# First modulation of a two-layer trunk: adaLN weights as TensorE's stationary operand, and the opening written out anew

## The chip, the cores and the metric

One Trainium2 chip, one of its cores. The time of a kernel is the device time of one launch in microseconds (us), given as the median of several runs; before and after are compared on it.

## What is computed

The program is a two-layer diffusion trunk (layer 0 an mLSTM mixer, layer 1 latent attention, a gated ConvFFN after each) on 256 latent and 256 context tokens of width 1024. Each sub-layer reads its input through a modulation that depends on a condition vector, `c` for the latent tokens and `c_ctx` for the context:

```python
def _modulation(cond, w, b):
    m = jax.nn.silu(cond) @ w + b          # (1024,) @ (1024, 6*1024)
    return jnp.split(m[:, None, :], 6, axis=-1)

def _modulate(x, shift, scale):
    return x * (1 + scale) + shift
...
ml = _modulation(c, ada_w[i], ada_b[i])
mc = _modulation(c_ctx[None, :], ada_w[i], ada_b[i])
hl = _modulate(x, ml[0], ml[1])
hc = _modulate(xc, mc[0], mc[1])
...
x_m = h @ w_up                             # the mLSTM's first product
```

The change touches only the first of these: shift and scale of layer 0, two times 1024 numbers for each of the two conditions, and the first product behind them, `h @ w_up`. Nothing of layer 0 can begin before shift and scale are there.

## The kernel before

All products of float32 data are made on TensorE from a rounded type (`F32R`): an operand is split into a high part (a cast on ScalarE, called ACT in the profile) and a low part (a subtraction on VectorE, called DVE), and three products high*high, high*low, low*high are summed. A matmul of plain `F32` operands also exists and needs no split.

**The opening** (`start_up`) computes shift and scale and the first `NUP` = 6 of the 16 column blocks of `h @ w_up`. It goes by eight blocks of 128 features, f = 0 to 7. For a block it loads the weights of the modulation (`adaw`), the transposed tokens `xT` (128 features x 512 tokens), and a row block `raw0` of `w_up` (128 x 768). Then:

- `rows`: the product of the conditions with the block's modulation weights. The two condition columns are the stationary operand and the weights stream, so the result `adar` is a row, two (or, split in high and low, four) partitions high. For f = 0 and 1 (`F32T`) the operands are plain float32; for the others the weights are split first (`hi` on ACT, `lo` on DVE, into `adas`) and the split condition `condr` is used.
- For f < `NFD` = 4, shift and scale of the block both come from these rows (256 columns); for f of 4 and above only the shift does (128 columns), and the scale comes from two multiply-and-sum instructions on DVE (`sum`, line L589) over a transposed copy `adat`.
- `copy` takes the row out of PSUM, `T` transposes it on TensorE back into PSUM, and `cols` adds the bias, which gives columns `mod0`, one number per feature and condition.
- `h` and `xx` apply shift and scale to the tokens (`h` rounded into `hT`, `xx` in float32), once for each half g of the tokens; `hlo` makes the low part. `whi` and `wlo` split the block of `w_up`.
- `up`f,i: the i-th of the three products of block f, six matmuls of 128 x 512, one into each of six PSUM banks that stay open through the opening. There are 8 x 3 x 6 = 144 of them (L745).

The order in which these steps are put on TensorE, DVE, ACT and SP's load queue is written out by hand, in the list `PLAN`; each engine then runs its own instructions in that order. SP's queue holds the loads of f = 0 to 3, the two condition rows `bc`, the loads of f = 4, and those of f = 5, 6, 7, which come when `wlo`0, 1, 2 stand in the list. Behind the opening comes `w_up`, the remaining ten column blocks (L458 to L460), and then the rest of the trunk, whose order a scheduler makes.

`Z`n issues n matmuls of a zero tile (L723), which compute nothing; `Z7` stands at the head of the list.

Of the kernel before, what the change touches and what calls it, by code (L numbers as in the profile page):

```python
# [8 lines left out]
F32R = mybir.dt.float32r  # L9
I32 = mybir.dt.int32  # L10
AF = mybir.ActivationFunctionType
ALU = mybir.AluOpType
# [5 lines left out]
T = SEQ + CTX  # L18
# [13 lines left out]
NB, NRAW, NU, NS = 3, 3, 31, 15  # L32
# [16 lines left out]

NUP = 6  # L50
NFD = 4
F32T = (0, 1)
PLAN = """
Z7 rows00 rows01 whi0 wlo0 copy0 T0 rows10 cols0 h00 h01 xx00 xx01 rows11 hlo0 up02 copy1 whi1 hi200 T1
up00 cols1 h10 hi210 lo200 up01 h11 wlo1 whi2 up10 lo210 hi300 rows20 wlo2 hi310 rows21 lo300 up12 copy2
lo310 whi3 xx11 T2 rows30 cols2 xx10 h21 rows31 h20 xx21 xx20 wlo3 up22 copy3 hi400 hlo2 T3 hlo1 silu0
up21 cols3 h30 silu1 lo400 up11 whi4 sum40 h31 rows40 hi500 sum41 up20 xx31 copy4 lo500 up32 whi5 xx30
hlo3 T4 rows50 cols4 wlo4 h41 up31 h40 sum50 hi600 up30 xx40 lo600 xx41 up42 copy5 hlo4 hi700 rows60 sum51
T5 up41 cols5 lo700 h51 copy6 up40 whi6 wlo5 xx51 sum60 rows70 h50 T6 sum61 copy7 up52 xx50 hlo5 up50
cols6 wlo6 h60 T7 up51 h61 sum70 whi7 xx60 up62 sum71 xx61 cols7 up60 hlo6 h70 wlo7 h71 up61 xx70 xx71  # L60
up72 hlo7 up70 up71
""".split()

TAIL = {"mout": 4, "aout": 7, "fout1": 6}
# [365 lines left out]
class K:  # L430
# [63 lines left out]
    def setup(self):  # L494
        nc, p = self.nc, self.pool
        a = self.a
        self.sm = p.tile([128, a["sm"].shape[1]], F32, name="sm")
        nc.sync.dma_start(self.sm[:, :32], a["sm"][:, :32])
        b1 = self.smc("ada_b")[:, 8:16]
        nc.vector.tensor_scalar(b1, b1, 1.0, None, op0=ALU.add)  # L500
        jp = p.tile([128, 128], I32, tag="s2", name="jp", bufs=NS)
        nc.gpsimd.iota(jp, pattern=[[1, 128]], base=0, channel_multiplier=-1)
        self.ident = p.tile([128, 128], F32, name="ident")
        nc.vector.tensor_scalar(self.ident, jp, 0.0, None, op0=ALU.is_equal)
        self.mask = p.tile([128, 2, 128], F32, name="mask")
        nc.vector.tensor_scalar(self.mask[:, 0], jp, 0.0, NEG, op0=ALU.is_gt, op1=ALU.mult)
        nc.vector.tensor_scalar(self.mask[:, 1], jp, 0.0, NEG, op0=ALU.is_lt, op1=ALU.mult)
        self.k1 = p.tile([128, 1], F32, name="k1")
        nc.vector.memset(self.k1, 1.0)
        self.zero = p.tile([128, 512], F32R, tag="s2", name="zero", bufs=NS)  # L510
        nc.vector.memset(self.zero.bitcast(F32), 0.0)
        self.keps = p.tile([128, 1], F32, name="keps")
        nc.vector.memset(self.keps, EPS)
        self.cond = p.tile([128, 8, 2], F32, name="cond")
        nc.scalar.activation(self.cond.rearrange("p a b -> p (a b)"), self.smc("cond"), AF.Silu)
        self.condr = p.tile([128, 8, 4], F32R, name="condr")
        self.split(self.condr[:, :, 0:2], self.condr[:, :, 2:4], self.cond)
        self.mod0 = p.tile([128, 2, 8, 2], F32, name="mod0")
        self.modc = {(0, c): self.mod0[:, c] for c in range(2)}
        self.gd = {}  # L520
        self.adav = p.tile([128, 32], F32, name="adav")
        nc.vector.memset(self.adav, 0.0)
        for l in range(2):
            for c in (3, 4) if l == 0 else (0, 1, 3, 4):
                self.modc[l, c] = p.tile([128, 8, 2], F32, name="mod%d%d" % (l, c))
            for c in (2, 5):
                self.gd[l, c] = self.dr.tile([2, D], F32, name="gd%d%d" % (l, c))

    def ada_hi(self, f, h, q):
        self.adas[f, h] = [self.pool.tile([128, 1024], F32R, tag="u", name="adas", bufs=NU) for _ in range(2)]  # L530
        self.nc.scalar.copy(self.adas[f, h][0], self.adaw[f, h])

    def ada_lo(self, f, h, q):
        hi, lo = self.adas[f, h]
        self.nc.vector.tensor_sub(lo, self.adaw.pop((f, h)), hi)

    def ada_rows(self, f, h):

        nc = self.nc
        nh = 2 if f < NFD else 1  # L540
        n = 128 * nh
        if h == 0:
            self.adap[f] = self.ps("adar")
        pr = self.adap[f]
        m = 8 // nh
        for k in range(h * m, (h + 1) * m):
            c = slice((k - h * m) * n, (k - h * m + 1) * n)
            if f in F32T:
                nc.tensor.matmul(pr[0:2, 0:n], self.cond[:, k, :], self.adaw[f, h][:, c], start=k == 0, stop=k == 7)
                continue  # L550
            for i, x in enumerate(self.adas[f, h]):
                nc.tensor.matmul(pr[0:4, 0:n], self.condr[:, k, :], x[:, c],
                                 start=k == 0 and i == 0, stop=k == 7 and i == 1)
        del (self.adaw if f in F32T else self.adas)[f, h]

    def ada_copy(self, f):
        n = 256 if f < NFD else 128
        q = 2 if f in F32T else 4
        self.adar[f] = r = self.s2("adarow")
        (self.nc.vector.tensor_copy if f == 0 else self.nc.scalar.copy)(r[0:q, 0:n], self.adap[f][0:q, 0:n])  # L560

    def ada_T(self, f):
        r = self.adar.pop(f)
        q = 2 if f in F32T else 4
        for i in range(2 if f < NFD else 1):
            self.nc.tensor.transpose(self.adap[f][:, 256 + q * i:256 + q * i + q], r[0:q, i * 128:(i + 1) * 128],
                                     self.ident[0:q, 0:q])

    def ada_cols(self, f):
        nc = self.nc  # L570
        p = self.adap.pop(f)[:, 256:]
        b = self.smc("ada_b").rearrange("p (c f) -> p c f", c=2)[:, :, f:f + 1]
        if f in F32T:
            nc.vector.tensor_tensor(self.mod0[:, :, f, :], p[:, 0:4].rearrange("p (c b) -> p c b", c=2),
                                    b.to_broadcast([128, 2, 2]), op=ALU.add)
            return
        n = 2 if f < NFD else 1
        m = self.mod0[:, 0:n, f, :]
        p = p[:, 0:4 * n].rearrange("p (c x b) -> p c x b", c=n, x=2)
        nc.vector.tensor_tensor(m, p[:, :, 0], b[:, 0:n].to_broadcast([128, n, 2]), op=ALU.add)  # L580
        nc.vector.tensor_tensor(m, p[:, :, 1], m, op=ALU.add)

    def ada_sum(self, f, j):

# [101 lines left out]
    def start_up(self):  # L686

        nc, st = self.nc, self.st
# [3 lines left out]
        self.t2d = {(p, j): self.dr.tile([128, 1024], F32, name="t2d") for p in range(2) for j in range(4)}  # L692
        self.xA, self.x1, self.xc, self.xcr = {}, {}, [], []
        w, raws = [], []
        self.adaw, self.adas, self.adap, self.adar, self.adat, self.xT = {}, {}, {}, {}, {}, []

        def load(f):
            if f < NFD:
# [57 lines left out]
        def silu(j):  # L756
            nc.scalar.activation(self.bc[j], self.bc[j], AF.Silu)

        ops = {"Z": warm, "rows": self.ada_rows, "copy": self.ada_copy, "T": self.ada_T, "cols": self.ada_cols,
               "hi": self.ada_hi, "lo": self.ada_lo, "sum": self.ada_sum, "silu": silu, "whi": w_hi, "wlo": w_lo,  # L760
               "h": h, "xx": lambda f, g: self.mod_part(f, g, self.xT[f]), "hlo": hlo, "up": up}
        e = mybir.EngineType
        with self.tc.manual_schedule(engines={e.PE, e.DVE, e.Activation, e.SP}):
# [4 lines left out]
            for t in PLAN:  # L768
                name = t.rstrip("0123456789")
# [1500 lines left out]
```

## Time and profile before

| | us |
|---|---|
| time, median of 3 runs | 1356.97 (1356.48 to 1357.79) |
| the profiled execution's own time | 1356.08 |
| its span in the profile | 1354.3 |
| from the first matmul that computes something to the first of `w_up` | 5.18 to 57.14 |

The profiled execution took 1.78 us more than its span, and 0.89 us less than the median. In the profile PE is TensorE's matmuls, PEld its loads of the stationary operand, SPq the load queue of SP. A plain float32 matmul leaves two records of a load and a matmul each in the trace, one of the rounded type leaves one. In the columns of a group, out<-in names the tiles, then come partitions x elements; for TensorE "128*2" stands for rows x columns of the stationary operand, and the shape behind it is what streams or is loaded. The ends of matmuls are modelled, so how fast they follow each other is read from their starts.

### The profile page before, as it was taken

What the parts mean: (1) busy time and instruction counts of PE and PEld (TensorE: products, weight loads), DVE (VectorE), ACT (ScalarE), POOL (GpSimd) and SP (SyncE); (2) the same over time, 40 slices, a digit from 0 to 9 for tenths busy, and PEclk for the clock granted to TensorE, in tenths of its full rate; (3) what the DMA queues carried; (4) which work ended last, traced back from release to release, by engine and by line L of the source; (5) the groups of instructions that cost most, each with busy time, mean ns of one, the idle gap of its engine ahead of it and who ended that gap; (6) DMA issues with size and microseconds to landing.
All of it is one profiled execution on the core that took longest, in us unless ns stands there. A gap on an engine that the chain in (4) does not pass through costs nothing.

```text
span 1354.3 us, 18733 instructions
## 1 busy us (share of the span) xinstructions
PE 1342.8 (99%) x6649; PEld 1126.8 (83%) x6649; DVE 1081.7 (80%) x1786; ACT 716.4 (53%) x1249; POOL 123.1 (9%) x216
## 2 busy tenths in 40 slices
PE   9999999999999999999999999999999999999997
PEld 6888888888788888888898888888888988988886
DVE  6898866687688696877789887778887898898884
ACT  5685443435444455374654333343458757676661
POOL 0032000011011010120002000000100011000100
PEclk9999999999999999999999999999999999999999
DMA  9799848789656373765747677775877425476850
GB/s 366 241 302 311 293 171 262 233 281 297 230 191 205 124 233 116 244 200 184 236 142 259 217 249 224 244 228 170 246 262 246 133 74 165 140 219 200 263 189 31
DMA packets 88093, 291.96 MB, mean 216 GB/s; under 512 B 11640, under 2 KB 12280, under 8 KB 88000
## 3 DMA queue, kind: packets, MB, share of 16 engines
q1 hardware_dynamic: 61840, 215.64, 48.7%
q0 software_dynamic: 17520, 57.70, 13.8%
q10 hardware_dynamic: 8640, 17.44, 3.4%
q8 instruction: 52, 0.85, 0.3%
q14 instruction: 41, 0.34, 0.1%
HBM read 260.15 MB, written 30.58 MB: 215 GB/s over the span
## 4 chain that ended last, share of the span: by engine, by line
PE 92%; DMA 4%; DVE 2%; ACT 1%; issue 0%; SPq 0%; DVEq 0%; ACTq 0%
PE fin L459 6%; PE fin L460 6%; PE fin L458 6%; PE tok L459 6%; PE tok L460 6%; PE tok L458 6%; PE y L1667 5%; PE fin L1578 5%; PE qk L458 4%; PE qk L460 4%; PE qk L459 4%; PE y L459 4%; PE y L458 4%; PE y L460 4%; PE fin L1583 3%; DMA raw<-in_ws 2%
## 5 line engine op out<-in xcount | busy, mean ns | idle before, releaser
L374 DVE TENSOR_TENSOR w<-raw,w 128x1024 fp32r<-128x1024 f32 (+1 forms) x256 | 307.5, 1205 | 111.4 <-ACT w L371 109.1
L371 ACT CAST w<-raw 128x1024 fp32r<-128x1024 f32 (+1 forms) x256 | 265.3, 1038 | 244.7 <-PE tok L460 86.3
L610 DVE SCALAR_TENSOR_TENSOR junk<-ar,bc 128x1024 f32<-128x1024 f32 x128 | 155.8, 1217 | 7.3 <-ACT bc L647 5.0
L459 PE MATMUL fin<-h,w 128*128 128x512 f32 (+1 forms) x376 | 141.2, 376 | 0.0
L458 PE MATMUL fin<-h,w 128*128 128x512 f32 (+1 forms) x376 | 141.2, 376 | 0.0
L460 PE MATMUL fin<-h,w 128*128 128x512 f32 (+1 forms) x376 | 141.1, 375 | 0.0
L458 PE MATMUL qk<-xc,w 128*128 128x512 f32 x256 | 100.5, 392 | 0.0
L460 PE MATMUL qk<-xc,w 128*128 128x512 f32 x256 | 99.7, 390 | 0.0
L459 PE MATMUL qk<-xc,w 128*128 128x512 f32 x256 | 99.6, 389 | 0.0
L459 PEld LDWEIGHTS fin<-h,w 128*128 128x128 f32 x376 | 70.8, 188 | 13.0
L458 PEld LDWEIGHTS fin<-h,w 128*128 128x128 f32 x376 | 70.7, 188 | 13.0
L460 PEld LDWEIGHTS fin<-h,w 128*128 128x128 f32 x376 | 70.7, 188 | 12.6
L1578 PE MATMUL fin<-h,w 128*128 128x512 f32 x312 | 78.1, 392 | 0.0
L1578 PEld LDWEIGHTS fin<-h,w 128*128 128x128 f32 x312 | 56.1, 189 | 10.0
L458 PEld LDWEIGHTS qk<-xc,w 128*128 128x128 f32 x256 | 48.1, 188 | 10.1 <-issue 0.4
L460 PEld LDWEIGHTS qk<-xc,w 128*128 128x128 f32 x256 | 48.0, 188 | 10.1
L459 PEld LDWEIGHTS qk<-xc,w 128*128 128x128 f32 x256 | 48.1, 188 | 9.8
L784 ACT ACTIVATE fg<-fg 128x512 f32<-128x512 f32 (+1 forms) x44 | 23.0, 525 | 58.7 <-DVE fg L782 52.5
L458 PE MATMUL tok<-w,hT 128*128 128x512 f32 x128 | 49.8, 389 | 0.0
L459 PE MATMUL tok<-w,hT 128*128 128x512 f32 x128 | 49.8, 389 | 0.0
L460 PE MATMUL tok<-w,hT 128*128 128x512 f32 x128 | 49.8, 389 | 0.0
L1667 PE MATMUL y<-w,fz 128*128 128x512 f32 x198 | 46.2, 392 | 0.4 <-DVE w L374 0.4
(495 smaller groups left out, 3257.0 us busy)
## 6 DMA issues: line engine op xcount, KB each, us to landing
raw<-in_ws SPq DMA_DIRECT2D x281, 512.0 KB, 4.7
ar<-in_adaT SPq DMA_DIRECT2D x80, 512.0 KB, 4.6
raw<-in_ws POOLq DMA_DIRECT2D x13, 512.0 KB, 7.7
raw<-in_ws SPq DMA_DIRECT2D x12, 384.0 KB, 8.3
adaw<-in_adaf SPq DMA_DIRECT2D x8, 512.0 KB, 6.6
xmd<-xr POOLq DMA_DIRECT2D x16, 256.0 KB, 4.9
xcd<-cv POOLq DMA_DIRECT2D x16, 256.0 KB, 5.6
xs<-xmd POOLq DMA_DIRECT2D x16, 256.0 KB, 6.4
```

What stands on the lines that cost most here:

```text
L371: k.nc.scalar.copy(h[:, :cols], src)
L374: k.nc.vector.tensor_sub(l[:, :cols], src, h[:, :cols])
L458: mm(out, w[0], x[0], start=start, stop=False)
L459: mm(out, w[0], x[1], start=False, stop=False)
L460: mm(out, w[1], x[0], start=False, stop=stop)
L610: nc.vector.scalar_tensor_tensor(o, w, 1.0, self.bc[j], op0=ALU.mult, op1=ALU.mult, accum_out=col[:, k, j:j + 1])
L784: nc.scalar.activation(tmp[:, :n], tmp[:, :n], AF.Silu)
L1578: nc.tensor.matmul(ps, w[0][:, c], hT(k), start=k == 0, stop=False, skip_group_check=True)
L1583: nc.tensor.matmul(ps[:, :n], w[1][:, k * 128:(k + 1) * 128], hT(k)[:, :n], start=False, stop=k == 7, skip_group_check=True)
L1667: nc.tensor.matmul(ps[b], a[:, p, ts], w[q][:, cs], start=j == 0 and n == 0 and not more, stop=j == end and n == 2, skip_group_check=True)
```

## The change

The modulation's weights become the stationary operand, in plain float32, 128 x 128 at a time, and the two condition columns stream. The result is at once a column per feature. Splits (`hi`, `lo`), row copies and transposes are gone for all eight blocks, with `condr` and the tiles `adas`; `cols` is a single addition for each block.

```diff
     def ada_rows(self, f, h):
 
         nh = 2 if f < NFD else 1
         if h == 0:
+            self.adap[f] = self.ps("adac")
+        w = self.adaw.pop((f, h))
         m = 8 // nh
         for k in range(h * m, (h + 1) * m):
-            c = slice((k - h * m) * n, (k - h * m + 1) * n)
-            if f in F32T:
-                nc.tensor.matmul(pr[0:2, 0:n], self.cond[:, k, :], self.adaw[f, h][:, c], start=k == 0, stop=k == 7)
-                continue
-            for i, x in enumerate(self.adas[f, h]):
-                nc.tensor.matmul(pr[0:4, 0:n], self.condr[:, k, :], x[:, c],
-                                 start=k == 0 and i == 0, stop=k == 7 and i == 1)
+            for c in range(nh):
+                i = (k - h * m) * nh + c
+                self.nc.tensor.matmul(self.adap[f][:, 2 * c:2 * c + 2], w[:, i * 128:(i + 1) * 128], self.cond[:, k, :],
+                                      start=k == 0 and c == 0, stop=k == 7 and c == nh - 1, skip_group_check=True)
...
     def ada_cols(self, f):
         n = 2 if f < NFD else 1
+        p = self.adap.pop(f)[:, 0:2 * n].rearrange("p (c b) -> p c b", c=n)
+        b = self.smc("ada_b").rearrange("p (c f) -> p c f", c=2)[:, 0:n, f:f + 1]
+        self.nc.vector.tensor_tensor(self.mod0[:, 0:n, f, :], p, b.to_broadcast([128, n, 2]), op=ALU.add)
...
-Z7 rows00 rows01 whi0 wlo0 copy0 T0 rows10 cols0 h00 h01 xx00 xx01 rows11 hlo0 up02 copy1 whi1 hi200 T1
+Z7 rows00 rows01 Z5 whi0 cols0 h00 h01 xx00 xx01 up00 wlo0 hlo0 up02 up01 whi1 rows10 rows11 rows20 cols1 h10 h11
...
```

`ada_hi`, `ada_lo`, `ada_copy` and `ada_T` are removed. A call of `ada_rows` for f < 4 is now 8 matmuls (two calls for a block), for f of 4 and above 8 in its one call, 96 in all.

The list `PLAN` is written anew. On TensorE, the opening stood like this before, from its first matmul on (`adar` are the condition's products and transposes, `up<-zero` the zero matmuls, `up<-hT,w` the 144):

```order
L723 MATMUL up<-zero 128x512 x7
L549 MATMUL adar<-adaw,cond 2x256 x8
L566 MATMUL adar<-ident,adarow 128x2 x2
L549 MATMUL adar<-adaw,cond 2x256 x8
L745 MATMUL up<-hT,w 128x512 x6
L566 MATMUL adar<-ident,adarow 128x2 x2
L745 MATMUL up<-hT,w 128x512 x18
L552 MATMUL adar<-adas,condr 4x256 x16
L745 MATMUL up<-hT,w 128x512 x6
L566 MATMUL adar<-ident,adarow 128x4 x2
L552 MATMUL adar<-adas,condr 4x256 x16
L745 MATMUL up<-hT,w 128x512 x6
```

Now it stands like this on TensorE (`adac` are the condition's products, the lines are those of the changed file):

```order
L683 MATMUL up<-zero 128x512 x7
L534 MATMUL adac<-cond,adaw 128x2 x16
L683 MATMUL up<-zero 128x512 x5
L705 MATMUL up<-hT,w 128x512 x18
L534 MATMUL adac<-cond,adaw 128x2 x32
L705 MATMUL up<-hT,w 128x512 x12
L534 MATMUL adac<-cond,adaw 128x2 x16
L705 MATMUL up<-hT,w 128x512 x36
L534 MATMUL adac<-cond,adaw 128x2 x16
L705 MATMUL up<-hT,w 128x512 x18
L534 MATMUL adac<-cond,adaw 128x2 x8
L705 MATMUL up<-hT,w 128x512 x24
```

All three products of block 0 now stand ahead of the condition's products of block 1, those of blocks 1 and 2 stand together, and five zero matmuls lie between the products of block 0 and the first `up`; behind the last row there are 8 more of the condition's and 36 more of the 144.

On SP's queue, the loads of blocks 5 and 6 stood like this before (`ar` is a tile of the modulation weights that belongs to work behind the opening):

```order
L711 DMA xT<-in_tokT 128x512
L716 DMA raw_185<-in_ws 128x768
L633 DMA ar<-in_adaT 128x1024
L705 DMA adaw<-in_adas 128x1024
L707 DMA adat<-in_adaT 128x1024
```

and like this now, with the loads of block 7 and what follows them:

```order
L671 DMA xT<-in_tokT 128x512
L676 DMA raw_207<-in_ws 128x768
L665 DMA adaw<-in_adas 128x1024
L667 DMA adat<-in_adaT 128x1024
L671 DMA xT<-in_tokT 128x512
L676 DMA raw_261<-in_ws 128x768
L665 DMA adaw<-in_adas 128x1024
L667 DMA adat<-in_adaT 128x1024
L671 DMA xT<-in_tokT 128x512
L676 DMA raw_298<-in_ws 128x768
L593 DMA ar<-in_adaT 128x1024 x3
```

One load of `ar` moved from ahead of block 6 to behind block 7; the loads otherwise keep their order. Behind the opening, the instructions of every engine stand in the order they had.

More of the change, by code (lines that the diff above doesn't have):

```diff
@@ L51 @@
 NFD = 4
-F32T = (0, 1)
 PLAN = """
-Z7 rows00 rows01 whi0 wlo0 copy0 T0 rows10 cols0 h00 h01 xx00 xx01 rows11 hlo0 up02 copy1 whi1 hi200 T1
[L55 to L61, printed above, removed]
+Z7 rows00 rows01 Z5 whi0 cols0 h00 h01 xx00 xx01 up00 wlo0 hlo0 up02 up01 whi1 rows10 rows11 rows20 cols1 h10 h11
+wlo1 rows21 up10 cols2 h20 h21 xx10 whi2 up12 xx21 wlo2 rows30 rows31 up20 cols3 h30 h31 xx30 xx31 xx20 up22
+whi3 hlo3 up30 wlo3 silu1 up31 xx11 silu0 hlo1 up32 sum40 up11 sum41 whi4 rows40 hlo2 rows50 cols4 wlo4 h41
+up21 h40 sum50 xx40 up40 xx41 sum51 whi5 up42 cols5 wlo5 h51 h50 rows60 hlo4 xx51 sum60 up50 xx50 sum61 up52
+cols6 hlo5 up41 h61 whi6 up51 h60 sum70 xx61 xx60 rows70 sum71 whi7 up60 cols7 hlo6 h70 wlo6 xx70 up61 h71
+xx71 up70 hlo7 wlo7 up62 up71 up72
 """.split()
@@ L515, in setup @@
         nc.scalar.activation(self.cond.rearrange("p a b -> p (a b)"), self.smc("cond"), AF.Silu)
-        self.condr = p.tile([128, 8, 4], F32R, name="condr")
-        self.split(self.condr[:, :, 0:2], self.condr[:, :, 2:4], self.cond)
         self.mod0 = p.tile([128, 2, 8, 2], F32, name="mod0")
@@ L527, in setup @@
                 self.gd[l, c] = self.dr.tile([2, D], F32, name="gd%d%d" % (l, c))
[L529 to L535, printed above, removed]
     def ada_rows(self, f, h):
-        nc = self.nc
         nh = 2 if f < NFD else 1
-        n = 128 * nh
@@ L542, in ada_rows @@
         if h == 0:
-            self.adap[f] = self.ps("adar")
-        pr = self.adap[f]
+            self.adap[f] = self.ps("adac")
+        w = self.adaw.pop((f, h))
         m = 8 // nh
         for k in range(h * m, (h + 1) * m):
-            c = slice((k - h * m) * n, (k - h * m + 1) * n)
-            if f in F32T:
-                nc.tensor.matmul(pr[0:2, 0:n], self.cond[:, k, :], self.adaw[f, h][:, c], start=k == 0, stop=k == 7)
-                continue
-            for i, x in enumerate(self.adas[f, h]):
-                nc.tensor.matmul(pr[0:4, 0:n], self.condr[:, k, :], x[:, c],
-                                 start=k == 0 and i == 0, stop=k == 7 and i == 1)
@@ L554, in ada_rows @@
[L554 to L567, printed above, removed]
@@ L569, in ada_cols @@
-    def ada_cols(self, f):
[L570 to L576, printed above, removed]
+            for c in range(nh):
+                i = (k - h * m) * nh + c
+                self.nc.tensor.matmul(self.adap[f][:, 2 * c:2 * c + 2], w[:, i * 128:(i + 1) * 128], self.cond[:, k, :],
+                                      start=k == 0 and c == 0, stop=k == 7 and c == nh - 1, skip_group_check=True)
@@ L577, in ada_cols @@
+    def ada_cols(self, f):
         n = 2 if f < NFD else 1
[L578 to L581, printed above, removed]
+        p = self.adap.pop(f)[:, 0:2 * n].rearrange("p (c b) -> p c b", c=n)
+        b = self.smc("ada_b").rearrange("p (c f) -> p c f", c=2)[:, 0:n, f:f + 1]
+        self.nc.vector.tensor_tensor(self.mod0[:, 0:n, f, :], p, b.to_broadcast([128, n, 2]), op=ALU.add)
@@ L694, in start_up @@
         w, raws = [], []
-        self.adaw, self.adas, self.adap, self.adar, self.adat, self.xT = {}, {}, {}, {}, {}, []
+        self.adaw, self.adap, self.adat, self.xT = {}, {}, {}, []
         def load(f):
@@ L757, in silu @@
             nc.scalar.activation(self.bc[j], self.bc[j], AF.Silu)
-        ops = {"Z": warm, "rows": self.ada_rows, "copy": self.ada_copy, "T": self.ada_T, "cols": self.ada_cols,
-               "hi": self.ada_hi, "lo": self.ada_lo, "sum": self.ada_sum, "silu": silu, "whi": w_hi, "wlo": w_lo,
+        ops = {"Z": warm, "rows": self.ada_rows, "cols": self.ada_cols, "sum": self.ada_sum, "silu": silu, "whi": w_hi, "wlo": w_lo,
                "h": h, "xx": lambda f, g: self.mod_part(f, g, self.xT[f]), "hlo": hlo, "up": up}
```

## The prediction, before any run of the changed kernel

> **What bounds the kernel now.** I read first the table of busy times by stretch, with the opening (5.1 to 57.1 us), the body and the tail apart. Columns: length, then busy us and instruction count of PE, PEld, DVE, ACT and POOL, then the granted TensorE clock, the DMA share and GB/s.
>
> ```profile
> 5.10:57.10 52.00, 51.01 (x284) 36.80 (x285) 39.16 (x70) 33.35 (x53) 0.00 (x0) 1.00 0.89 335
> 57.10:1340.00 1282.90, 1281.56 (x6313) 1081.58 (x6313) 1031.71 (x1689) 679.90 (x1190) 119.85 (x209) 1.00 0.66 213
> 1340.00:1354.30 14.30, 6.88 (x48) 6.25 (x46) 9.49 (x20) 1.41 (x3) 2.84 (x2) 0.87 0.19 73
> ```
>
> PE rests 1.0 us in the opening and 1.3 us in the whole body. Two things follow. The opening is bound by what stands on PE, not by ACT (33 of 52 us) or DVE (39). And as the body's order is unchanged and PE has hardly a gap there, a shift of the opening's end reaches the end of the program nearly whole, with either sign.
>
> Then the timeline of PE through the opening (start, length, engine, line):
>
> ```profile
> 1.49 3.36 PE L723 MATMUL up<-zero 128*128 128x512 f32 x7 [1.49 <-DVE adav L522]
> 5.18 3.88 PE L549 MATMUL adar<-adaw,cond 128*2 128x256 f32 x16 [0.34 <-DMA adaw<-in_adaf]
> 9.91 0.28 PE L566 MATMUL adar<-ident,adarow 2*128 2x2 f32 x2 [0.85 <-DVE adarow L560]
> 10.13 3.62 PE L549 MATMUL adar<-adaw,cond 128*2 128x256 f32 x16
> 13.67 1.65 PE L745 MATMUL up<-hT,w 128*128 128x512 f32 x6
> ...
> 19.67 2.01 PE L552 MATMUL adar<-adas,condr 128*4 128x256 f32 x16
> ...
> 29.61 1.12 PE L552 MATMUL adar<-adas,condr 128*4 128x128 f32 x16
> ...
> 47.13 10.17 PE L745 MATMUL up<-hT,w 128*128 128x512 f32 x42
> 57.14 0.39 PE L458 MATMUL up<-hT,w 128*128 128x512 f32 x1
> ```
>
> The opening lasts from 5.18 to 57.14, 51.96 us. Its 144 `up` matmuls follow each other every 0.238 us (42 of them from 47.13 to 57.14), 34.3 us in all. The other 17.7 us are the condition's products, their transposes and two short waits. The change replaces these 17.7 us.
>
> **What goes.** On ACT and DVE, the split of the modulation weights:
>
> ```profile
> L535 DVE TENSOR_TENSOR adas<-adaw,adas 128x1024 fp32r<-128x1024 f32 x8 | 9.7, 1221 | 2.0 <-ACT adas L531 2.0
> L531 ACT CAST adas<-adaw 128x1024 fp32r<-128x1024 f32 x8 | 8.3, 1048 | 4.3 <-DMA adaw<-in_adas 3.4 <-DMA adaw<-in_adaf 0.9
> ```
>
> 18 us of work, and I count it at nothing: PE was the bound while they ran. The seven row copies go the same way, except the first, behind which PE waited 0.85 us. On PE the 17.7 us go.
>
> **What comes, and its unknown.** 96 matmuls of plain float32 with a 128x128 stationary operand and two streaming columns. The order lists 8 plain products where the trace has 16 records, so these are 192 pairs of load and matmul. Two streaming columns cost next to nothing; a pair costs what a load of 128 columns costs. The kernel before has no such pair, so I bound it by the nearest loads, in groups by shape (last but one: mean ns of one):
>
> ```profile
> L549 PEld LDWEIGHTS adar<-adaw,cond 128*2 128x2 f32 x32 | 2.6, 86 | 4.9 <-issue 1.5
> L552 PEld LDWEIGHTS adar<-adas,condr 128*4 128x4 f32 x96 | 6.5, 85 | 1.7 <-DVE adas L535 0.2
> L458 PEld LDWEIGHTS up<-hT,w 128*128 128x128 f32 x80 | 15.0, 188 | 3.1
> L1323 PEld LDWEIGHTS zT<-ident,z 128*128 128x128 f32 x64 | 7.4, 140 | 0.8
> ```
>
> All have some 85 ns that do not depend on the columns. The rounded type (L552 to L458) adds 103 ns for 124 columns, 0.83 ns a column, 106 ns for 128. The plain type, if the transposes of L1323 stand for it, adds 54 ns for 126 columns (L549 to L1323), 55 ns for 128. How closely such loads can follow shows in a stretch of plain transposes with 64 streaming columns:
>
> ```profile
> 403.21 0.22 PE L1030 MATMUL gt<-ident,B 64*128 64x64 f32 x1
> 403.27 0.22 PE L1029 MATMUL gt<-ident,ab 64*128 64x64 f32 x1
> ...
> 403.58 0.22 PE L1030 MATMUL gt<-ident,B 64*128 64x64 f32 x1
> ```
>
> Seven starts in 0.37 us, a pair every 0.062 us, each with its load of 128 columns: 7 ns over the 55. So a pair costs 0.062 us at the transposes' rate and 0.113 at the rounded type's. Which rate holds for a plain load that is not a transpose? The streaming side gives the hint:
>
> ```profile
> 1054.38 0.28 PE L460 MATMUL kn<-ckT,wu 128*128 128x256 f32 x1
> 1054.50 0.28 PE L458 MATMUL kn<-ckT,wu 128*128 128x256 f32 x1
> 1104.41 1.04 PE L2027 MATMUL PT<-ident,P 128*128 128x128 f32 x8
> ```
>
> The rounded type streams 256 columns in 0.12 us (0.47 ns a column). The plain products of L549 need 0.22 (16 from 10.13 to 13.67), 0.86 ns a column, and the plain transposes of L2027 at most 0.13 for 128, about 1.0 with the end of the last in it. On that side the plain product behaves as the plain transpose, not as the rounded type; so I take 0.062, and keep 0.113 as a rival.
>
> The Trainium skill ("TensorE: Matmul & The Clock Gate", the section on LDWEIGHTS) has one rule for every type, columns divided by 1.2, 107 ns for 128; its section on the weight path excludes FP32 from the fast load, and its list of terms sets the FP32 transpose apart as a faster mode. By it the pair would be the dear one, and the kernel slower. The trace agrees for the rounded type (106) and not for the transposes (55); no row shows the case itself.
>
> **The new opening, summed.** The start, from the timeline of all engines:
>
> ```profile
> 7.71 0.83 ACT L728 CAST w<-raw 128x768 fp32r<-128x768 f32 x1 [4.39 <-DMA raw<-in_ws]
> 10.43 0.60 ACT L679 ACTIVATE hT<-xT,mod 128x256 fp32r<-128x256 f32 x1 [1.89 <-DVE mod L574]
> ```
>
> Block 0's products begin at 5.18 as before, with their load: 32 pairs, 2.0 us, and 0.3 us because PE's clock comes up only then (the first 16 records of L549 took 3.88 us, the next 3.62): 7.4. The five zero matmuls (1.2 us) end at 8.6, inside a gap: `whi`0 on ACT waits for its load till 7.71, ends at 8.54, and `h`0 of the latent half behind it takes 0.60. First `up` at 9.2. From there PE has 34.3 us of `up` and 160 pairs, 9.9 us, if nothing is late: end at 53.4, against 57.14, so **3.7 us earlier**.
>
> Is anything late? The loads of the modulation weights, as their casts show when each had landed:
>
> ```profile
> 14.78 2.00 ACT L531 CAST adas<-adaw 128x1024 fp32r<-128x1024 f32 x2
> 18.65 1.05 ACT L531 CAST adas<-adaw 128x1024 fp32r<-128x1024 f32 x1 [0.65 <-DMA adaw<-in_adaf]
> 19.95 1.05 ACT L531 CAST adas<-adaw 128x1024 fp32r<-128x1024 f32 x1 [0.25 <-DMA adaw<-in_adaf]
> ...
> 31.05 1.04 ACT L531 CAST adas<-adaw 128x1024 fp32r<-128x1024 f32 x1
> ...
> 36.27 1.05 ACT L531 CAST adas<-adaw 128x1024 fp32r<-128x1024 f32 x1 [0.40 <-DMA adaw<-in_adas]
> ...
> 40.50 1.05 ACT L531 CAST adas<-adaw 128x1024 fp32r<-128x1024 f32 x1 [2.05 <-DMA adaw<-in_adas]
> ```
>
> By the new order PE asks for block 2's halves at 15.5 and 16.5 (there by 14.8 and 15.8), block 3's at 20.3 and 21.3 (18.65, 19.95), block 5 at 31.9 (31.05), 6 at 37.2 (36.27), 7 at 43.8 (40.50). The covers are 0.7 us and more, and blocks 6 and 7 come sooner, as a load of `ar` moved behind them. What that `ar` feeds stands behind the opening on DVE, so it hides. If a cover fails, its 0.5 us or so comes off the gain. ACT and DVE have less to do in the same order of blocks.
>
> The body passes the shift on, so the profiled execution becomes 1356.08 - 3.7 = 1352.4. The median lies 0.89 above the profiled execution; against it I forecast **1353.3**. Own range: pairs of 0.055 give 4.8 us; pairs of 0.070 with the first `up` 0.3 late and 0.4 us of small waits give 1.7. So 1352.2 to 1355.3.
>
> **Rivals.** *A, the dear load* (slower): a pair costs 0.113. Block 0's products end at 5.18 + 3.6 + 0.3 = 9.1, the zero matmuls at 10.3, then 34.3 and 160 x 0.113 = 18.1: end at 62.7, 5.6 us late, 1362.5. The point where gain turns into loss is a pair of 0.084. For it: the 188 ns of L458; against it: the plain type's streaming rate.
>
> *B, the load that doubles*: the plain type streams at half the rounded type's rate; if it also loads at half of it, or leaves more records than two, a pair is 0.22. Then 12.5, 13.7 with the zero matmuls, 34.3, 35.2: end at 83.2, 26.1 late, 1383.1. Against it: 2 columns of it (86 ns) cost no more than 4 of the rounded type (85).
>
> *C, the clock*: the first matmuls run slow, 3.36 us for 7 against 0.238 each, and by the 0.3 us above it takes from 1.49 to about 5.7 till the clock is full; in the tail, with PE at work less than half the time, the granted clock is 0.87. Blocks 1 and 2 now stand together, 64 pairs, 4.0 us in which two columns stream. If that counts as rest, the clock drops and some 4.2 us run at half speed, 2.1 lost; twice if the first block's products hold the clock down too. Of the 3.7 are left 1.6, or nothing and 0.5 us lost: 1355.4 to 1357.5. The Trainium skill (same page, Part 1) has a window of about 3.4 us for both directions; by it the start agrees with the trace, and 4.0 us are long enough for a drop, if light work counts as idle, which it does not say.
>
> **Numbers.** Forecast 0.54, A 0.25, C 0.12, B 0.09. What this kernel's measurement can tell from no change is about 0.2%, 2.7 us. Faster by more than that: most of the forecast, a little of C, 0.51. Within: the rest of both, 0.15. Slower: A and B, 0.34. The range 1352.0 to 1363.0 leaves out B and the dearer edge of A, some 0.15.
>
> **What will show it.** The spacing of the `adac` matmuls: 0.062 right, 0.11 is A, 0.22 is B. The first `up` at 9.2, the first matmul of `w_up` (L455) at 53.4. A granted clock under 1.00 in the opening would be C. The forecast is wrong in its second step if PE waits on loads or on `mod`, and in its last if the body gives the shift back.

## The result, and the profile after

| | before | after |
|---|---|---|
| median, us | 1356.45 (6 runs, 1354.53 to 1357.79) | 1372.52 (6 runs, 1366.81 to 1375.81) |
| the profiled execution's own time | 1356.08 | 1372.77 |
| its span | 1354.3 | 1371.0 |
| first matmul of `w_up` (end of the opening) | 57.14 | 71.75 |
| mean granted clock, over the runs | 0.998 to 0.999 | 0.989 to 0.993 |

The change makes the kernel slower: ratio 1.0116, 95% interval 1.0100 to 1.0132. Of the 16.7 us between the two spans, 14.6 arise in the opening. One run of the kernel before took 2178 us and one of the 32-column kernel below 4071 us, both slow all through; neither counts in any ratio.

The table of busy times by stretch of the changed kernel (opening, then body; columns as in the prediction's table):

```profile
5.10:71.70 66.60, 66.60 (x341) 58.66 (x342) 29.48 (x57) 24.25 (x38) 0.00 (x0) 0.82 0.70 260
71.70:1356.70 1285.00, 1282.98 (x6313) 1083.39 (x6313) 1031.55 (x1688) 679.76 (x1190) 119.84 (x209) 1.00 0.66 212
```

PE has no gap at all in the opening, so nothing was late there and PE alone sets its end. ACT and DVE are each 9 to 10 us lighter than in the table of before, and it brings nothing. The granted clock of the opening is 0.82 where it was 1.00. PE's timeline shows what fills it:

```profile
4.95 3.92 PE L534 MATMUL adac<-cond,adaw 128*128 128x2 f32 x32
8.73 2.48 PE L683 MATMUL up<-zero 128*128 128x512 f32 x5
11.01 4.62 PE L705 MATMUL up<-hT,w 128*128 128x512 f32 x18
15.47 10.86 PE L534 MATMUL adac<-cond,adaw 128*128 128x2 f32 x64
26.19 5.47 PE L705 MATMUL up<-hT,w 128*128 128x512 f32 x12
31.45 3.98 PE L534 MATMUL adac<-cond,adaw 128*128 128x2 f32 x32
35.29 10.03 PE L705 MATMUL up<-hT,w 128*128 128x512 f32 x36
45.15 3.63 PE L534 MATMUL adac<-cond,adaw 128*128 128x2 f32 x32
48.64 5.98 PE L705 MATMUL up<-hT,w 128*128 128x512 f32 x18
54.46 1.84 PE L534 MATMUL adac<-cond,adaw 128*128 128x2 f32 x16
56.16 5.75 PE L705 MATMUL up<-hT,w 128*128 128x512 f32 x24
61.75 1.84 PE L534 MATMUL adac<-cond,adaw 128*128 128x2 f32 x16
63.45 8.47 PE L705 MATMUL up<-hT,w 128*128 128x512 f32 x36
71.75 0.39 PE L455 MATMUL up<-hT,w 128*128 128x512 f32 x1
```

Read from start to start, 32 pairs take 3.49 us (45.15 to 48.64), 0.109 us each, and the last 36 `up` 8.30 us, 0.231 each. But 64 pairs from 15.47 take 10.72 us, 0.168 each, and 18 `up` from 48.64 take 5.82, 0.323 each. Some stretches run at another speed. The granted clock by stretches says which (the bounds were put near its changes):

```profile
8.30:11.70 3.40, 3.40 (x11) 2.82 (x11) 2.76 (x8) 1.20 (x2) 0.00 (x0) 0.50 1.04 417
11.70:18.50 6.80, 6.80 (x45) 6.09 (x45) 0.01 (x1) 0.83 (x1) 0.00 (x0) 1.00 1.04 410
18.50:32.10 13.60, 13.60 (x54) 12.44 (x54) 3.30 (x7) 2.43 (x4) 0.00 (x0) 0.50 1.03 403
32.20:35.50 3.30, 3.30 (x30) 3.30 (x31) 0.04 (x1) 0.00 (x0) 0.00 (x0) 1.00 1.02 400
35.60:39.00 3.40, 3.40 (x9) 2.65 (x8) 2.83 (x6) 3.30 (x6) 0.00 (x0) 0.50 1.03 405
49.30:52.60 3.30, 3.30 (x10) 2.53 (x9) 3.27 (x7) 2.68 (x6) 0.00 (x0) 0.50 0.44 149
```

Between 8.3 and 52.7 us the clock is at one half four times, for 3.41, 13.65, 3.41 and 3.41 us (multiples of 3.41), 23.9 us in all, which is some 12 us lost. Each fall comes after a stretch of pairs has filled most of 3.4 us, and the matmuls behind it pay.

The body adds 2.1 us more. The place is at 690 us; the stretch around it, and PE's waits in it:

```profile
690.00:694.00 4.00, 2.63 (x10) 1.30 (x9) 2.55 (x3) 3.45 (x5) 0.00 (x0) 1.00 0.38 122
694.00:698.00 4.00, 4.00 (x11) 3.14 (x12) 2.95 (x5) 1.25 (x2) 0.00 (x0) 0.57 0.88 279
```

```profile
691.44 0.49 PE L455 MATMUL y<-wu,hn 128*128 128x512 f32 x1 [0.31 <-ACT wu L356]
692.70 0.50 PE L456 MATMUL y<-wu,hn 128*128 128x512 f32 x1 [0.77 <-DVE wu L357]
693.96 0.50 PE L456 MATMUL y<-wu,hn 128*128 128x512 f32 x1 [0.30 <-DVE wu L357]
```

PE waits 1.4 us for a split of weights that landed late, and behind it the clock is at half once more, for 3.41 us, some 1.6 us lost. The body's shift against before, matmul by matmul, goes from 14.6 to 17.4 here and comes back to 16.6 by 1040 us.

### The profile page after: what moved, and what is told of

Read it like the earlier page. It is cut to its first block, busy times and chain, and to the rows that moved or that the text cites. A ratio compares the mean times of both kernels' runs of the same rounds, so it can differ in the third digit from the quotient of the medians.

```text
span 1371.0 us, 18806 instructions
## 1 busy us (share of the span) xinstructions
PE 1360.0 (99%) x6706; PEld 1150.7 (84%) x6706; DVE 1071.3 (78%) x1770; ACT 706.9 (52%) x1233; POOL 123.1 (9%) x216
## 4 chain that ended last, share of the span: by engine, by line
PE 98%; ACT 1%; DVE 1%; DMA 1%; issue 0%; DVEq 0%; ACTq 0%
PE y L1626 7%; PE fin L455 6%; PE fin L456 6%; PE tok L455 6%; PE fin L457 6%; PE tok L457 6%; PE tok L456 6%; PE fin L1537 5%; PE qk L455 4%; PE qk L457 4%; PE qk L456 4%; PE y L456 4%; PE y L457 4%; PE y L455 4%; PE up L705 3%; PE fin L1542 3%
```

## The experiments

Theory K was written down after this reading: a pair of load and plain product costs 0.112 us because of its load, and a stretch of pairs that stream only 2 columns each counts as rest, so that the clock falls. Rivals: L, the new list is at fault and not the products; S, load and stream don't overlap.

### 64 and 16 streaming columns

Both keep the changed kernel's list and loads. The condition columns are repeated, and only the first two of the result are used.

```diff
-self.nc.tensor.matmul(self.adap[f][:, 2 * c:2 * c + 2], w[...], self.cond[:, k, :], ...)
+self.nc.tensor.matmul(self.adap[f][:, 64 * c:64 * c + 64], w[...], self.condw[:, k, :], ...)
```

> The changed kernel, but 64 columns stream instead of 2 (the two condition columns 32 times over); only the first two of the result are used. The loads of the stationary operand stay the same. Theory K (two costs: a pair of load and matmul takes 0.112 us, and stretches in which hardly anything streams let the granted clock fall to a half): 64 plain columns stream in about 55 ns, inside the 112 of the pair, so PE has the same work and the clock stays at 1.00. The opening then ends near 4.95 + 32 x 0.112 + 1.2 + 34.3 + 160 x 0.112 = 62 (60.5 if the up matmuls keep the 0.2285 that they have after the change), 3.5 to 5 us later than in the kernel before: about 1360 to 1361.5, and the runs lie as close together as those before. Rival L (the new list makes the waits, or PE is slow for a reason that has nothing to do with what streams): still about 1372, clock 0.99. Rival S (stream and load don't overlap): pairs of 0.165 and more, about 1370 with a full clock.

> As the kernel with 64 streaming columns, but 16: some 14 ns of streaming in a pair of 112. Theory K says only that it lies between the changed kernel (2 columns, 1372) and the one with 64 (1360 to 1361.5): nearer to 1372 if an eighth of the time counts as rest, nearer to 1361 if it counts as work. I expect the clock to fall still, 1368. Rival L: 1372. Rival S: 0.12 a pair, 1362 to 1373 by the clock.

Measured with 64: 1363.57 (1359.89 to 1367.67, 4 runs; before 1356.02), ratio 1.0068 (1.0049 to 1.0088). With 16: 1370.97 (1369.25 to 1373.38), ratio 1.0114 (1.0098 to 1.0130). PE's timeline with 64:

```profile
14.15 7.25 PE L538 MATMUL adac<-condw,adaw 128*128 128x64 f32 x64
21.21 3.01 PE L709 MATMUL up<-hT,w 128*128 128x512 f32 x12
```

64 pairs take 7.06 us, 0.110 each, although 32 times as many columns stream: a pair costs its load, and the stream lies beside it. S falls. In this profile, which was taken of the shortest of the four runs, the clock stays at 1.00 from 5.4 us to the tail, and the opening ends at 60.81. The median lies above K's range, and the runs lie 7.8 us apart, which K doesn't explain; it is taken up below.

With 16 columns the clock is at half from 23.1 to 33.3 and from 36.7 to 43.5, and `w_up` begins at 73.89. Block 0's pairs are 0.213 us apart, so it was at half at the head too, till the first recorded rise at 16.2:

```profile
4.94 6.98 PE L538 MATMUL adac<-condw,adaw 128*128 128x16 f32 x32
11.76 2.48 PE L687 MATMUL up<-zero 128*128 128x512 f32 x5
```

### The condition stationary, in plain float32

The rows of the kernel before for all eight blocks, in plain float32 without a split, with its list: the matmuls are as plain as the changed kernel's, but 256 or 128 columns stream.

```diff
-F32T = (0, 1)
+F32T = tuple(range(8))
```

> The kernel before with all eight blocks' condition products in plain float32 rows, as blocks 0 and 1 have them there: the condition is the stationary operand, the weights stream, and the splits of the modulation weights on ACT and DVE are gone; copies and transposes stay, and the list is that of before without the splits. It removes the same work from ACT and DVE as the change, and keeps PE streaming. By the rows of before, blocks 2 and 3 cost 3.5 us on PE instead of 1.9, blocks 4 to 7 1.75 instead of 0.96: 6.4 us more. Theory K: clock 1.00, about 1362 to 1363, spread as before. Rival L or a theory by which the missing casts slow something else: as the change, about 1372.

Measured 1363.12 (1361.59 to 1365.37), ratio 1.0056 (1.0041 to 1.0071). The clock doesn't fall, and `w_up` begins at 64.05. So plain float32 as such does not lower the clock.

### The changed products in the list of before

```diff
-Z7 rows00 rows01 Z5 whi0 cols0 h00 h01 xx00 xx01 up00 wlo0 hlo0 up02 up01 whi1 rows10 rows11 rows20 ...
+Z7 rows00 rows01 whi0 wlo0 rows10 cols0 h00 h01 xx00 xx01 rows11 hlo0 up02 whi1 up00 cols1 h10 up01 h11 ...
```

> The change's products, but in the order of the list of before (its splits, copies and transposes left out): block 0 and 1 at the start together, 64 pairs or 7.2 us, then 32, 32, 16, 16, 16 and 16 pairs with 6 to 24 up matmuls between them. Theory K: the same 192 pairs, so 3 to 5 us over the kernel before by the loads alone, and at least the first stretch of 7.2 us lets the clock fall, later ones by chance: 1363 to 1370, with the runs apart by several us. Rival L (the new list is at fault): 1360 to 1361 with a full clock.

Measured 1375.62 (1372.59 to 1375.64), ratio 1.0141 (1.0126 to 1.0156): 3 us dearer than the new list. L falls, and K's own range was too low.

```profile
5.12 13.79 PE L534 MATMUL adac<-cond,adaw 128*128 128x2 f32 x64 [0.28 <-DMA adaw<-in_adaf]
18.77 7.86 PE L705 MATMUL up<-hT,w 128*128 128x512 f32 x24
```

The 64 pairs at the head take 13.65 us, 0.213 each: they run at half speed throughout, and the clock first rises at 23.3. Such pairs not only let the clock fall, they also don't raise it.

### 128 and 32 streaming columns

The columns are repeated by the access pattern, without a copy.

```diff
-self.cond[:, k, :]
+self.cond[:, k:k + 1, :].to_broadcast([128, 64, 2])
```

> The changed kernel with the two condition columns repeated 64 times, so that 128 columns stream behind each load; the list is the changed one. At 0.86 ns a column the stream takes 110 ns, about as long as the 113 ns between pairs that 64 columns showed, so TensorE streams nearly all the time. Theory K (a pair costs its load; thin streaming lets the clock fall): spacing 0.112 to 0.116 us, no fall of the clock in the opening of any run, w_up begins at 60.5 to 61.3, 1359.0 to 1361.0, and the runs lie within 2 us of each other, where those with 64 columns lay 8 apart. Rival S (load and stream don't overlap): spacing 0.22, 20 us more, 1380.

> As before it, with 32 columns (28 ns of stream in 113). Theory K gives no threshold: with 16 columns the clock fell as with 2, with 64 it held in the profiled run. If 28 of 113 counts as rest: 1367 to 1372 and half clock in several stretches of the opening; if it counts as work: 1359 to 1363.

With 128: 1360.89 (1359.79 to 1362.34, 5 runs; before 1355.77), ratio 1.0038 (1.0024 to 1.0051). Clock, median and end of the opening are as K said; the pairs stand 0.110 us apart, a little closer than it gave, and the runs lie 2.6 us apart, where it gave 2:

```profile
5.11 4.06 PE L534 MATMUL adac<-cond,adaw 128*128 128x128 f32 x32 [0.27 <-DMA adaw<-in_adaf]
14.30 7.30 PE L534 MATMUL adac<-cond,adaw 128*128 128x128 f32 x64
21.36 3.01 PE L706 MATMUL up<-hT,w 128*128 128x512 f32 x12
```

```profile
5.10:60.90 55.80, 55.79 (x341) 49.66 (x342) 29.07 (x54) 24.29 (x38) 0.00 (x0) 1.00 0.82 313
```

The same 341 matmul records that took 66.6 us take 55.8, at a granted clock of 1.00. That is the clock's share: 11 us of the opening, 11.6 of the medians. What is left, an opening end of 60.96 (3.8 late), is the price of the pairs. With 32 columns there is one run to read, 1368.19, without a profile; its mean clock of 0.993, against 0.998 to 0.999 with 128 columns, says that the clock fell.

### Pairs mixed among the `up` matmuls

The 2-column products of blocks 1 to 7 are cut in calls of 4 pairs (`q`) and put behind every 3 `up` (`a` and `b` are halves of `up`).

```diff
-... up00 wlo0 hlo0 up02 up01 whi1 rows10 rows11 rows20 ...
+... a00 q10 q11 b00 q12 q13 wlo0 hlo0 a02 q14 q15 b02 q16 q17 whi1 wlo1 cols1 h10 h11 a01 b01 ...
```

> The changed kernel's products with 2 columns, but the products of blocks 1 to 7 are put between the up matmuls, 4 pairs (0.45 us) after every 3 up (0.71 us), instead of 16 to 64 pairs in a row; block 0's 32 pairs stand together as they were. Theory K, with the clock going by the average over some 3.4 us: in such a mix matmuls that stream 512 columns fill more than half of each window, so no half clock behind 12 us; block 0's stretch may still cost up to 4 us. w_up begins at 60 to 64, 1360 to 1364. Rival N (loads in close succession lower the clock however they are mixed): half clock returns behind 12 us, 1368 or more.

Measured 1384.62 (1383.87 to 1386.82), ratio 1.0212 (1.0197 to 1.0226), the slowest of all. (8 pairs stand between 3 `up` in the trace: each `q` is 4 records, and two follow each other.) Neither theory had this. PE's timeline:

```profile
5.17 6.96 PE L537 MATMUL adac<-cond,adaw 128*128 128x2 f32 x32 [0.32 <-DMA adaw<-in_adaf]
...
18.53 1.70 PE L548 MATMUL adac<-cond,adaw 128*128 128x2 f32 x8
20.09 1.63 PE L721 MATMUL up<-hT,w 128*128 128x512 f32 x3
21.52 1.70 PE L548 MATMUL adac<-cond,adaw 128*128 128x2 f32 x8
...
34.27 0.94 PE L721 MATMUL up<-hT,w 128*128 128x512 f32 x3
35.05 0.95 PE L548 MATMUL adac<-cond,adaw 128*128 128x2 f32 x8
...
52.66 0.98 PE L721 MATMUL up<-hT,w 128*128 128x512 f32 x3 [1.50 <-ACT hT L655]
```

The same mix runs at half speed till 30 us (8 pairs and 3 `up` in 2.99 us) and at full speed from 30.5 on (1.59 us). The rise at 30.5 came behind nine `up` in a row (26.07 to 30.05). The mix holds the full clock, but doesn't reach it by itself. A wait of 1.50 us at 51 lowers it again, from 54.4 to 61.2, and one of 1.11 us at 68 from 71.5 to 78.3. So theory R: to rise, the clock needs a window of about 3.4 us that is nearly full; to fall, one that is less than about half full; in between it keeps what it has.

### The same mix, with block 0 wide

As above, with 128 streaming columns for block 0's products alone, and the `sum` steps put a block earlier, so that `h` is in time.

```diff
-for block 0: self.cond[:, k, :]
+for block 0: self.cond[:, k:k + 1, :].to_broadcast([128, 64, 2])
-... cols4 sum40 sum41 h40 h41 a32 b32 ...
+... xx30 xx31 sum40 sum41 a30 q40 ... cols4 h40 h41 a32 b32 ...
```

> The mixed kernel (2 columns, 4 pairs after every 3 up), with 128 streaming columns in block 0's products alone, and the sums over adat put earlier, so that PE doesn't wait for h. Theory R: block 0 now lets the clock rise at about 5 to 9 us; behind it the same mix that ran at half speed till 30.5 us, at 45 % of streaming, holds the full clock, since a window must be nearly idle to lower it. w_up begins at 60 to 62.5, 1359 to 1362. If a mix of 45 % is too thin by itself: half clock again, 1368 or more.

Measured 1361.11 (1359.00 to 1361.76, 5 runs; before 1356.37), ratio 1.0034 (1.0021 to 1.0048): 23 us less than the mix before it, within R's range.

```profile
4.94 3.94 PE L537 MATMUL adac<-cond,adaw 128*128 128x128 f32 x32
...
13.76 0.95 PE L549 MATMUL adac<-cond,adaw 128*128 128x2 f32 x8
14.57 0.94 PE L723 MATMUL up<-hT,w 128*128 128x512 f32 x3
15.35 0.95 PE L549 MATMUL adac<-cond,adaw 128*128 128x2 f32 x8
```

The mix that stood at half speed now runs at full speed through the whole opening, which ends at 60.93. With 2 columns, too, the clock's loss is gone. Two things were changed here, and weren't tried apart: the wide block 0 for the early stretch, the earlier sums for the falls at 54 and 71 us.

The wide block 0 did another thing in this profile than R had foreseen. The rise came at 5.22, behind the zero matmuls, which filled 89% of the 3.41 us before it; in the profile of the mix before it, whose list begins alike, they filled 48% of the window from 3.2 to 6.6, and it didn't rise. So here the wide block 0 is seen to hold the clock (in the changed kernel it fell at 8.29, behind the thin block 0), not to raise it. Where the windows lay isn't what parts the two kernels: their runs, 1359.00 to 1361.76 and 1383.87 to 1386.82, are far apart.

### A transpose against a product

In the kernel before, the eight transposes from which the prediction took its 0.062 us become ordinary products with the identity; operands, shapes and place stay.

```diff
-nc.tensor.transpose(pt[:, t * 64:(t + 1) * 64], ab[0:64, t * 128:(t + 1) * 128], self.ident[0:64, 0:64])
+nc.tensor.matmul(pt[:, t * 64:(t + 1) * 64], ab[0:64, t * 128:(t + 1) * 128], self.ident[0:64, 0:64], start=True, stop=True)
```

> The kernel before, in which the eight plain float32 transposes of the gates (tile gt, L1029 and L1030), from whose spacing of 0.062 us the price of a pair was taken, are written as ordinary products with the identity: the same operands, the same 64x128 stationary tile, the same 64 streaming columns. If the pair's price hangs on whether the matmul is a transpose (theory K): each now leaves two records, and their starts lie 0.11 us apart, 16 records in 1.7 us instead of 8 in 0.45. If it hangs on the shape (64 rows of the stationary tile instead of 128; rival H): two records each, 0.06 us apart. The time stays within 2 us of the kernel before.

One run, 1357.71 (before 1356.37). Its timeline at the place quoted in the prediction:

```profile
403.40 0.38 PE L1031 MATMUL gt<-ident,B 64*128 64x64 f32 x2
403.63 0.38 PE L1029 MATMUL gt<-ident,ab 64*128 64x64 f32 x2
403.85 0.38 PE L1031 MATMUL gt<-ident,B 64*128 64x64 f32 x2
404.07 0.38 PE L1029 MATMUL gt<-ident,ab 64*128 64x64 f32 x2
```

Each leaves two records, and the next begins 0.223 us later: 0.112 a pair where the transpose has 0.062. The load itself differs too, in the tile's own rows, first of this kernel, then of the kernel before (duration min, median, max in ns):

```profile
L1031 PEld LDWEIGHTS gt<-ident,B x8: 188/188/188, 403.3 to 404.8; 64*128 64x128 f32 x8
```

```profile
L1030 PEld LDWEIGHTS gt<-ident,B x4: 137/139/140, 403.2 to 403.5; 64*128 64x128 f32 x4
```

H falls: with 64 rows or 128, a product's load of 128 plain columns costs the dear price, and the cheap one belongs to the transpose.

### The spread with 64 columns

By R, 64 columns (55 ns of stream in 110) hold the clock, but can't raise it; where the first window behind the zero matmuls isn't full, block 0 and what follows run slow. With 14 zero matmuls at the head one window is always full. The second run is the kernel of 64 columns unchanged.

```diff
-Z7 rows00 rows01 Z5 whi0 cols0 ...
+Z7 Z7 rows00 rows01 whi0 cols0 ...
```

> The kernel with 64 streaming columns, with 14 zero matmuls at the head instead of 7, and without the 5 behind block 0's products. Theory R: the clock rises only at the end of a window of about 3.4 us that was busy throughout; the windows lie where they lie; and a stream of 64 columns in 113 ns holds the clock up but can't raise it. Then the runs of the kernel with 7 zero matmuls lie up to 8 us apart because in some the rise comes behind block 0 (about 16 us) instead of at 5.4. 14 zero matmuls (3.4 us at full clock, 6.7 at half) always hold a whole window: the first product begins at 6.5 to 8.3, the first up at 11 to 13, 1361 to 1363.5, and the runs lie within 3 us of each other. If the spread has another cause: again 8 us or so.

> The kernel with 64 streaming columns once more, for a second profile of it. Theory R: if its time is over 1362, the profile shows the records of block 0's products and of the ups behind them at half speed (pairs 0.21, up 0.45) till some 14 to 18 us; if it is near 1360, at full speed from 5 to 6 us on.

14 zero matmuls: 1362.31 (1361.57 to 1364.01, 4 runs), ratio 1.0047 (1.0030 to 1.0064), a spread of 2.4 us where it was 7.8. The second profile came out at 1360.18, with the clock up at 5.6 us. Both fit R, but none of the longer runs with 64 columns has a profile, so this cause of the spread, and that 64 columns can't raise the clock, are argued and not shown.

### A version against both kernels

The kernel before, with columns (128 streaming) for blocks 0 and 1 alone, where its products were plain anyway.

```diff
-Z7 rows00 rows01 whi0 wlo0 copy0 T0 rows10 cols0 h00 h01 xx00 xx01 rows11 hlo0 up02 copy1 whi1 hi200 T1
+Z7 rows00 rows01 whi0 cols0 h00 h01 wlo0 rows10 xx00 xx01 rows11 hlo0 up02 whi1 hi200
```

> The kernel before, with its list, in which only blocks 0 and 1 (plain float32 before too) are made as columns, 128 of them streaming; blocks 2 to 7 keep their rows in the rounded type. For these two blocks the products cost the same either way (32 pairs of 0.113 are 3.6 us, as their rows took), and two row copies, two transposes (0.28 us each) and PE's wait of 0.85 us go: up to 1.4 us less, 1354.6 to 1356.3 beside about 1356.0, if the splits of block 2 are in time; nothing if they are late.

Measured 1355.60 (1354.42 to 1356.23, 11 runs; before 1355.77), ratio 0.9996 (0.9987 to 1.0005): better than the change by some 16 us, not distinguishable from the kernel before. In its profile `w_up` begins at 56.39, 0.75 us earlier.

## Why the prediction was wrong

**What bounds it: right.** PE has no gap in the opening, and the body passes the opening's shift on unchanged till 640 us (14.6). The loads were nowhere late; but PE came later to each of them than foreseen, so the covers weren't put to the test.

**The failed step is the price of a pair.** It took 0.062 us, by the transposes' rate, because plain products stream at the transposes' rate. The trace of after and every kernel with these products has 0.109 to 0.112, rival A's price. That the streaming rates agree says nothing of the loads: the same operands cost 0.062 as a transpose and 0.112 as a product. The rule of the Trainium skill that the prediction set against its own choice, columns divided by 1.2, so 107 ns for 128 ("TensorE: Matmul & The Clock Gate", the section on LDWEIGHTS), agrees with the product (0.109 to 0.112 us) and not with the transpose (0.062 us). The Trainium skill's list of terms on that page sets the FP32 transpose apart as a faster mode. The prediction, which cites this too, priced the product by the transpose all the same. The kernel with 128 streaming columns gives the sum without the clock's part: its opening ends at 60.96 where 53.4 was forecast, 7.6 late. Its terms: 192 pairs of 0.110 instead of 0.062, 9.2 more; 144 `up` at 0.231 instead of 0.238, 1.0 less; and the gap before the first `up`, 0.6, which the longer pairs fill. Rival B falls with it: the 0.213 us of some pairs resembles its 0.22, but the same pairs stand 0.109 apart in the stretches at full clock.

**Rival C came on top, and was mis-sized.** It was priced at 2.1 us, or twice that, and as an alternative to A; the two came together, and dear pairs make the thin stretches longer, so each made the other worse: 192 pairs of 0.11 are 21 us of thin work, not 12. The stretches at half clock were 23.9 us, and the opening lost 11 us by them. The Trainium skill's window of about 3.4 us ("TensorE: Matmul & The Clock Gate", Part 1) agrees with the 3.41 us of which all these stretches are multiples. That stretches of thin work lower the clock although PE never rests, these runs show.

**The body** was to pass the shift on, and added 2.1 us. The late weights at 690 us also show with 64 and 128 columns (the shift grows there by 1.3 and 1.4 us, and by 0.4 in the second profile of 64), but not with the plain rows; why the load comes later there wasn't tried. The half clock behind it is theory R's: of the 3.41 us before the fall, `y`'s matmuls, 0.23 us each, filled about 40%, and PE waited for much of the rest.

The range ended at 1363.0, because its cases stood side by side: A alone, or C alone. A and C together, with A's 62.7 and the 11 us, would have been 1373.5; with C's own 2.1 to 4.2 us it would have been 1364.6 to 1366.7, outside the range too, and still short of what was measured.

## What to carry to other kernels

Making the weights stationary for a handful of streaming columns turns TensorE's work into loads: count 0.11 us for each pair of load and plain float32 product (two pairs for each matmul), whatever streams up to 128 columns, and don't price it from transposes. Then look at what such a stretch does to the clock: where a product streams little for 3 us and more, fill the same time with repeated columns, which cost nothing beside the load (with 128 of them the mean granted clock was 0.998 to 0.999 in all five runs, with 16 it was 0.991 to 0.993), or put it between dense matmuls behind a clock that is already up. No version with columns was measurably faster than the rows in the rounded type, whose stationary operand is 4 columns wide. And ask of two rivals whether they exclude each other, or whether one feeds the other.

## What the runs showed of the hardware

**The clock's two thresholds.** In the openings recorded here the changes of the granted clock lie whole multiples of 3.41 us apart. From PE's timelines, these are the shares of such a window that matmuls of 512 columns took, where the rest was pairs of 2 or 16 columns or a wait.

| | share of the window, kernel and place in us |
|---|---|
| PE busy throughout, the clock fell | 5% (changed products in the list of before, 26.7 to 30.1), 11% (after, 15.1 to 18.5), 18% (after, 45.8 to 49.2) |
| PE busy throughout, it stayed up | 41% (16 columns, 50.4 to 53.8), 46% (the mix, 30.5 to 33.9), 49% (the mix with block 0 wide, 12.0 to 15.5) |
| PE partly idle, it fell | 33% (the mix, 51.0 to 54.4, idle 44%), 46% (the mix, 68.1 to 71.5, idle 30%) |
| it didn't rise | 43 to 61% (the mix, 10.0 to 27.1), 62% (16 columns, 36.7 to 40.1), 69% (changed products in the list of before, 30.1 to 33.6), 76% (after, 25.4 to 28.8) |
| it rose | 79% (after, 28.8 to 32.2) and more |

The same 46% held the clock with pairs beside it and lost it with a wait beside it, so this share isn't the whole measure: the thin pairs seem to count for a little. Pairs of 128 columns count for more: in the kernel of the last experiment the clock rose at 6.95, behind a window with 38% of zero matmuls and 57% of such pairs. All these shares are read from the traces; only the pair of mixes was an experiment on them. Nor do the windows begin with the program: in the kernel before and in its copy with products for the gates' transposes, whose openings are the same, the first recorded change is at 5.75 and at 7.68.

**Where the clock column is blind.** The granted clock reads 1.00 until its first recorded change. The mix's stretch at half speed and the one at full speed stand in its table like this:

```profile
14.20:30.40 16.20, 16.20 (x57) 14.10 (x55) 4.27 (x8) 2.04 (x4) 0.00 (x0) 1.00 1.03 405
30.60:50.00 19.40, 19.40 (x125) 17.40 (x125) 6.46 (x13) 5.75 (x8) 0.00 (x0) 1.00 0.70 255
```

Both say 1.00, and in the first PE gets 57 matmul records through in 16.2 us, in the second 125 in 19.4. The mean clock of a run has the same blind spot. At a program's start the spacing of records of one kind is the witness, not the clock.
